# Half of the DMAs of a running logsumexp moved from SyncE's queue to ScalarE's

## The chip, the cores and the metric

The kernel runs on one core of a Trainium2 chip. A core has five engines that run their own instruction streams and meet at semaphores: TensorE (matrix multiply, into PSUM), VectorE, ScalarE (activation functions), GpSimd and SyncE, which computes nothing and here only issues DMAs. Sixteen DMA engines move data between HBM and the on-chip SBUF (128 partitions). SyncE and ScalarE can each issue DMAs through a hardware queue of their own; the issuing instruction hands the transfer over and the engine goes on, while the transfer runs. An engine executes its instructions in order: one that waits holds up all behind it.

The metric is the time of one execution on the device in microseconds. Three runs of the kernel before gave 1262.69, 1262.9 and 1263.4 us; the median is 1262.9.

## The reference

`x` has the shape (4, 4096, 4128) in float32: 4 batches, 4096 time steps, 4128 columns. The output is the running logsumexp along time, for each batch and column:

```python
out[:, 0, :] = x[:, 0, :].copy()
for t in range(1, S):
    mx = np.maximum(out[:, t - 1, :], x[:, t, :])
    out[:, t, :] = mx + np.log(np.exp(out[:, t - 1, :] - mx) + np.exp(x[:, t, :] - mx))
```

That is log(cumsum(exp(x))) along time. Input and output are 270.5 MB each, and each byte has to be moved once.

## The kernel before

**Tiles.** The work is cut into 44 steps (`steps`, lines 185 to 195), each with one tile of its own, so that "tile 21" is that of step 21. A step takes 384 consecutive time rows of one batch, all 4128 columns; 4096 = 10 x 384 + 256, so each batch has ten steps of three rows a partition (`r` = 3) and one of two (`r` = 2, first in batch 0, last in the others). Counting from 0, the two-row steps are 0, 21, 32 and 43. Partition p holds `r` consecutive time rows, a contiguous piece of HBM of 49,536 bytes (33,024 in a two-row step). One DMA loads a whole step (`Step.load`, line 127), one stores it (`Step.store`, line 130). Results are written in place: the tile `xt` is loaded, replaced by its exponentials in float16 (in half of the same bytes) and then by the logarithms in float32, and stored. Four such buffers exist (`bufs = 4`).

**Chunks.** A step is cut into four chunks of 1024 columns; the fourth has the tail of 32 columns too. For each chunk:

- `exp` (line 142, ScalarE): exponentials of all `r` rows of the chunk in one instruction.
- `head` (lines 92 and 96, TensorE): matrix products with triangular constants add up, in PSUM, the exponentials of all earlier rows of the step for row j = 0, and the carry from the step before (`pick` times `carry`).
- `stage(j)` (line 175, ScalarE): the logarithm of the PSUM sum goes to the tile as the output of row j. Then, for j + 1 < r, TensorE adds the next row's exponentials (`ident`). After the last row `keep` (lines 106 and 107, VectorE) saves the new carry. The tail's 32 columns have a logarithm of their own (line 180) behind stage 0 of the fourth chunk.

**Order.** The order is written out by hand (`tc.manual_schedule()`); the framework adds the semaphores. The main loop (line 205) goes through rounds g. Round g does stage 2 of chunk g - 2, stage 1 of chunk g - 1 and stage 0 of chunk g (three logarithms on ScalarE), then the exponential of chunk g + 2 and the head of chunk g + 1. When a step's last chunk has had its last stage, within the round and ahead of the remaining stages, the step is stored and the next load is issued (lines 210 to 214): with step s stored, the load of step s + 3. That load goes to the buffer of step s - 1, so it waits until the store of step s - 1 has landed. By then the exponentials of step s + 1 are all done but the last chunk's; ScalarE needs step s + 2 in the round after.

**Queues.** All loads and stores are issued by SyncE (`nc.sync.dma_start`) on one hardware queue, in the order store s, load s + 3, store s + 1, load s + 4. The first four loads are issued at the start. In the profile the exponentials are L142, the logarithms L175 and L180, loads L127, stores L130. Where a line of code calls TensorE through the helper `mm`, the profile has L92 (with a change of weights) or L96.

Of the kernel before, what the change touches and what calls it, by code (L numbers as in the profile page):

```python
# [49 lines left out]
def kernel(  # L50
# [11 lines left out]
    nc = tc.nc  # L62
# [49 lines left out]
    class Step:  # L112
# [7 lines left out]
            rows = t[self.b, self.row:self.row + P * self.r, :]  # L120
            return rows.rearrange("(p j) d -> p j d", j=self.r)

        def load(self):
            full = xpool.tile([P, R, D], FP32, name="xt")
            self.xt = full[:, :self.r, :]
            self.half = self.xt.bitcast(FP16)
            nc.sync.dma_start(out=self.xt, in_=self.dram(x))  # L127

        def store(self):
            nc.sync.dma_start(out=self.dram(out), in_=self.xt)  # L130

    class Chunk:
        def __init__(self, step, c):
# [51 lines left out]
    steps = []  # L185
# [10 lines left out]

    chunks = [Chunk(s, c) for s in steps for c in range(n_main)]
    ahead = bufs - 1
    for s in steps[:bufs]:
        s.load()  # L200
    stored = 0
    chunks[0].exp()
    chunks[1].exp()
    chunks[0].head()
    for g in range(len(chunks) + R - 1):
        for d in range(R - 1, -1, -1):
            if 0 <= g - d < len(chunks) and d < chunks[g - d].t.r:
                k = chunks[g - d]
                k.stage(d)
                if k.c == last and d + 1 == k.t.r:  # L210
                    k.t.store()
                    if bufs <= stored + ahead < len(steps):
                        steps[stored + ahead].load()
                    stored += 1
        if g + 2 < len(chunks):
            chunks[g + 2].exp()
        if g + 1 < len(chunks):
            chunks[g + 1].head()
# [30 lines left out]
```

## Time and profile before

| | |
|---|---|
| median of three runs | 1262.9 us |
| span of the profiled execution, first to last instruction | 1261.0 us |
| moved to and from HBM | 541 MB, 429 GB/s over the span |
| ScalarE busy | 947.0 us |
| TensorE busy | 690.7 us |
| VectorE busy | 451.4 us |
| a load of a three-row step, issue to landing (median of 40) | 42.2 us |
| a store of a three-row step, issue to landing (median of 40) | 28.1 us |
| exp of one chunk, ScalarE (mean of 176) | 2.72 us |
| log of one row of one chunk, ScalarE (mean of 512) | 1.03 us |

The profiled execution has no time of its own besides its span; the 1.9 us between the span and the median of the runs lie outside the first and last instruction, or are the difference between executions.

How to read the lines: an instruction line names its place in the program (L142), the engine, the operation and the tiles, output first. "SPq" is SyncE's queue of instructions, which here are all DMA issues. A transfer's landing is the time when the last of the 16 DMA engines reports its part done. "A <- B" in a table of waits says that A stood idle until B was done. The DMA share is the mean busy share of the 16 DMA engines.

### The profile page before, as it was taken

Reading aid. Unit: us, or ns where it says so; the run is one execution under the profiler, and the core shown is the slowest. Engines: PE = TensorE matmul, PEld = TensorE weight load, DVE = VectorE, ACT = ScalarE, POOL = GpSimd, SP = SyncE. Lnnn points to the kernel's source line nnn. Section 1 sums busy time; section 2 is a strip of 40 time slices with the busy share of each in tenths; the row PEclk is TensorE's granted clock in tenths of the full one; section 3 lists DMA queues with packets and bytes.
Section 4 is the critical chain, followed back from the end, with each engine's and each line's share of the span. In section 5 each row is a group of like instructions: output and inputs, shape, how many; then the busy total and the mean of one; then the engine's idle time right before and its main releaser. Section 6 shows DMA issues by size and latency. Waiting matters only on the chain.

```text
span 1261.0 us, 6165 instructions
## 1 busy us (share of the span) xinstructions
PE 690.7 (55%) x2268; PEld 236.3 (19%) x2268; DVE 451.4 (36%) x445; ACT 947.0 (75%) x733; POOL 2.2 (0%) x13
## 2 busy tenths in 40 slices
PE   3666545565565555555346655555534755555562
PEld 1222111121121111111112221211211211111120
DVE  2443333333333333334424333333442433333344
ACT  5997777777777777778569777777866977777784
POOL 0000000000000000000000000000000000000000
PEclk9987787877777777878778777777777778787776
DMA  9999999999999999999999999999999999999998
GB/s 411 411 443 428 432 429 437 431 431 434 437 429 431 431 439 431 434 427 434 436 431 433 434 431 438 430 434 432 435 431 433 437 430 434 433 434 431 433 420 348
DMA packets 12702, 541.46 MB, mean 429 GB/s; under 512 B 1408, under 2 KB 1408, under 8 KB 1408
## 3 DMA queue, kind: packets, MB, share of 16 engines
q1 hardware_dynamic: 12672, 541.07, 99.4%
q8 instruction: 18, 0.29, 0.1%
q14 instruction: 12, 0.10, 0.0%
HBM read 270.53 MB, written 270.53 MB: 429 GB/s over the span
## 4 chain that ended last, share of the span: by engine, by line
DMA 72%; ACT 19%; PE 5%; issue 2%; DVE 1%; SPq 0%; ACTq 0%
DMA xt<-in_x_dram 67%; ACT xt L142 10%; ACT xt L175 9%; DMA out_dram<-xt 5%; PE pt L96 3%; PE pt L92 2%; DVE carry L106 0%; DVE carry L107 0%; ACT xt L180 0%; SPq L130 0%; ACTq L244 0%; SPq L127 0%; ACTq L142 0%; PE qt L92 0%
## 5 line engine op out<-in xcount | busy, mean ns | idle before, releaser
L142 ACT ACTIVATE xt<-xt 128x3072 f16<-128x3072 f32 (+3 forms) x176 | 478.2, 2717 | 247.9 <-DMA xt<-in_x_dram 247.8
L175 ACT ACTIVATE xt<-pt 128x1024 f32<-128x1024 f32 x512 | 487.3, 1029 | 2.5 <-PE pt L96 0.7
L106 DVE CAST carry<-pt 32x1024 f16<-32x1024 f32 x176 | 216.5, 1230 | 760.9 <-ACT xt L175 760.7
L92 PE MATMUL pt<-xt,ident 128*128 128x512 f16 x176 | 76.6, 435 | 493.7 <-ACT xt L175 493.7
L96 PE MATMUL pt<-xt,ident 128*128 128x512 f16 x496 | 203.7, 477 | 35.4 <-ACT xt L175 34.7
L107 DVE TENSOR_TENSOR carry<-pt,carry 32x1024 f16<-32x1024 f32 x176 | 215.8, 1226 | 6.1
L96 PE MATMUL pt<-xt,excl 128*128 128x512 f16 x496 | 187.6, 496 | 0.0
L96 PEld LDWEIGHTS <-ident 128*128 128x128 f16 x496 | 51.0, 103 | 655.0 <-issue 641.3
L92 PE MATMUL pt<-xt,incl 128*128 128x512 f16 x176 | 92.2, 524 | 23.5 <-ACT xt L142 15.1
L92 PE MATMUL pt<-xt,excl 128*128 128x512 f16 x176 | 93.4, 531 | 0.0
L96 PE MATMUL pt<-xt,incl 128*128 128x512 f16 x176 | 92.9, 528 | 0.0
L96 PEld LDWEIGHTS <-excl 128*128 128x128 f16 x536 | 66.6, 124 | 104.1 <-issue 79.5
L92 PE MATMUL pt<-carry,pick 128*128 128x512 f16 x160 | 72.0, 450 | 0.0
L96 PE MATMUL pt<-carry,pick 128*128 128x512 f16 x160 | 68.5, 428 | 0.0
L180 ACT ACTIVATE xt<-qt 128x96 f32<-128x96 f32 (+1 forms) x44 | 10.9, 248 | 46.3 <-PE pt L96 46.3
L92 PEld LDWEIGHTS <-incl 128*128 128x128 f16 x220 | 22.6, 103 | 118.0 <-DVE carry L107 95.3
L92 PEld LDWEIGHTS <-excl 128*128 128x128 f16 x220 | 26.8, 122 | 36.8 <-issue 27.9
L96 PEld LDWEIGHTS <-incl 128*128 128x128 f16 x260 | 27.8, 115 | 10.9 <-issue 4.8
L92 PEld LDWEIGHTS <-pick 128*128 128x128 f16 x200 | 22.9, 114 | 30.4 <-issue 20.4
L96 PEld LDWEIGHTS <-pick 128*128 128x128 f16 x160 | 18.4, 115 | 28.6 <-issue 17.2
L92 PEld LDWEIGHTS <-ident 128*128 128x128 f16 x176 | 19.2, 109 | 22.7 <-issue 12.8
L106 DVE CAST carry_t<-qt 32x32 f16<-32x32 f32 x44 | 8.7, 197 | 26.0 <-ACT xt L180 25.8
(21 smaller groups left out, 56.5 us busy)
## 6 DMA issues: line engine op xcount, KB each, us to landing
xt<-in_x_dram SPq DMA_DIRECT2D x40, 6192.0 KB, 42.2
out_dram<-xt SPq DMA_DIRECT2D x40, 6192.0 KB, 28.1
xt<-in_x_dram SPq DMA_DIRECT2D x4, 4128.0 KB, 37.3
out_dram<-xt SPq DMA_DIRECT2D x4, 4128.0 KB, 29.6
```

The source lines that it names most:

```text
L92: nc.tensor.matmul(pt, lhsT=w, rhs=rhs, start=start, stop=stop, skip_group_check=True)
L96: pe.add_instruction(mybir.InstMatmult(name=nc.get_next_instruction_name(), ins=[pe.lower_ap(rhs), pe.lower_ap(w, for_matmul_weights=True) ...
L106: nc.vector.tensor_copy(cr[HI:HI + 32, :], pt[HI:HI + 32])
L107: nc.vector.tensor_tensor(out=cr[LO:LO + 32, :], in0=pt[HI:HI + 32], in1=cr[HI:HI + 32, :], op=mybir.AluOpType.subtract,)
L142: nc.scalar.activation(self.t.half[:, :, 2 * c0:2 * c0 + w], self.t.xt[:, :, c0:c0 + w], ACT.Exp,)
L175: nc.scalar.activation(t.xt[:, j, c * CH:(c + 1) * CH], pt, ACT.Ln)
L180: nc.scalar.activation(t.xt[:, :, t0:D], self.qt, ACT.Ln)
```

## The change

SyncE issues the first four loads and, while fewer than 22 steps are stored (`stored < half`), all stores and loads: stores 0 to 21 and loads 4 to 24. From store 22 on ScalarE issues, on its own hardware queue: stores 22 to 43 and loads 25 to 43. A store keeps its place in program order, behind the last stage of its step. A load issued by SyncE comes at the end of the stages of the same round; a load issued by ScalarE comes two rounds (two chunks) later, behind that round's three logarithms and ahead of its exponential. Nothing in the arithmetic is touched.

```diff
-        def load(self):
+        def load(self, queue):
             full = xpool.tile([P, R, D], FP32, name="xt")
             self.xt = full[:, :self.r, :]
             self.half = self.xt.bitcast(FP16)
-            nc.sync.dma_start(out=self.xt, in_=self.dram(x))
-
-        def store(self):
-            nc.sync.dma_start(out=self.dram(out), in_=self.xt)
+            queue.dma_start(out=self.xt, in_=self.dram(x))
+
+        def store(self, queue):
+            queue.dma_start(out=self.dram(out), in_=self.xt)
...
     ahead = bufs - 1
+    half = len(steps) // 2
+    queue = lambda: nc.sync if stored < half else nc.scalar
+    stored = 0
     for s in steps[:bufs]:
-        s.load()
-    stored = 0
+        s.load(nc.sync)
+    due = {}
...
                 if k.c == last and d + 1 == k.t.r:
-                    k.t.store()
+                    k.t.store(queue())
                     if bufs <= stored + ahead < len(steps):
-                        steps[stored + ahead].load()
+                        due[g if stored < half else g + 2] = (steps[stored + ahead], queue())
                     stored += 1
+        if g in due:
+            s, q = due.pop(g)
+            s.load(q)
         if g + 2 < len(chunks):
             chunks[g + 2].exp()
```

## The prediction

> **What bounds the kernel now.** I read the page first: busy times, the slices, the queues.
>
> ```profile
> span 1261.0 us, 6165 instructions
> ...
> PE 690.7 (55%) x2268; PEld 236.3 (19%) x2268; DVE 451.4 (36%) x445; ACT 947.0 (75%) x733; POOL 2.2 (0%) x13
> ...
> DMA  9999999999999999999999999999999999999998
> ...
> q1 hardware_dynamic: 12672, 541.07, 99.4%
> ```
>
> No compute engine is full; ScalarE, the fullest, works 75% of the span. The 16 DMA engines are at nine tenths or more in all slices but the last, and all 541 MB go through one hardware queue. Next come the waits: who stands still, and for what. The first line is ScalarE's, the other two are SyncE's queue.
>
> ```profile
> ACT xt L142 <- DMA xt<-in_x_dram: 247.8, 42, 11.8
> ```
>
> ```profile
> SPq L130 <- ACT xt L175: 1174.4, 44, 30.0
> SPq L127 <- DMA out_dram<-xt: 18.4, 5, 4.9
> ```
>
> ScalarE is late for nothing but loads: 247.8 us in 42 waits, 5.9 us a step. A load almost never waits for the store that frees its buffer (5 times, 4.9 us at most). Then SyncE's timeline around the middle, each line a start and a duration.
>
> ```profile
> 632.86 0.33 SPq L130 DMA_DIRECT2D out_dram<-xt  x1
> 638.10 0.34 SPq L127 DMA_DIRECT2D xt<-in_x_dram  x1
> 668.50 0.33 SPq L130 DMA_DIRECT2D out_dram<-xt  x1
> 668.93 0.38 SPq L127 DMA_DIRECT2D xt<-in_x_dram  x1
> ...
> 751.28 0.33 SPq L130 DMA_DIRECT2D out_dram<-xt  x1
> 751.71 0.38 SPq L127 DMA_DIRECT2D xt<-in_x_dram  x1
> 780.60 0.33 SPq L130 DMA_DIRECT2D out_dram<-xt  x1
> ```
>
> Counting from the first, the store at 632.86 is that of tile 21 (tiles count from 0), so 668.50 is tile 22, the first that ScalarE would issue, and 638.10 is the load of tile 24. In the steady stretch stores are 29.32 us apart (751.28 to 780.60): one store and one load, 14.65 us each. Forty such pairs and four pairs of two-row tiles (9.76 us a transfer, from the completion of store 42 at 1250.40 to that of store 43 at 1260.16) take 40 x 29.3 + 4 x 19.5 = 1250 us of the 1261. The data path is the bound, and issue order or issuer can only matter where the path runs dry. The end of the program shows such a place, in busy times by stretch (last columns: DMA share, GB/s).
>
> ```profile
> 1220.00:1230.00 10.00, 6.13 (x25) 2.28 (x25) 3.46 (x6) 8.18 (x8) 0.00 (x0) 0.83 0.89 386
> 1230.00:1240.00 10.00, 6.41 (x20) 2.06 (x20) 7.79 (x7) 9.60 (x9) 0.00 (x0) 0.83 0.63 269
> ```
>
> The mean DMA engine is idle 1.1 + 3.7 = 4.8 us there, because the engines have drifted apart: store 41 completes on its first engine at 1227.96 and on its last at 1235.55, and store 42 was issued at 1234.00. The last engine was never dry; it sets the end.
>
> **The change, part by part.** The profiled execution spans 1261.0 us; the runs' median is 1262.9. The sum is made on the span and 1.9 us are added.
>
> *First half.* Stores and loads 0 to 24 stay on SyncE (load 24 is still due at store 21). Loads now stand after the remaining stages of the same round in program order, but SyncE runs none of these: 0.
>
> *Steady second half, on the queue.* Take store 25 at 751.28. Ahead of it is load 27, which lands at 764.68 (from the trace's completion records, one for each of the 16 engines, as all landings here); store 25 then runs until 779.4. Load 28 is issued today at 751.71 and lies in the queue until then. After the change it comes two rounds later: after ScalarE has received load 27, run one exp and three logs (5.5 us; the rows at 677.02 to 682.52 below), and perhaps the tail's log, which waits 0.68 to 1.10 us for TensorE: 6.4 us in all. 764.7 + 6.4 = 771.1, plus 0.38 of issuing and 1.0 until the first bytes move (the first load of the program: issued at 0.80, first packet at 1.81) is 772.5. The path needs it at 779.4. Cover 6.9 us, cost 0. If that cover were gone, each microsecond would be paid on each of the 19 loads that ScalarE issues (25 to 43). The store that frees the buffer is issued a step earlier and lands 28.1 us after its issue (the median of the page's DMA part); ScalarE asks for it 49 us after that issue (store 24 at 722.04, load 28 at 771.1), so this wait holds nothing.
>
> *Steady second half, on ScalarE.* A store is the instruction behind the log that finishes its tile, ahead of two more logs. ScalarE stands from the end of that log: 0.04 us to the issue (the log's row of 1232.93 and 1.02 us, the store at 1234.00), 0.33 of issuing, some 0.06 to start again (the chain has 0.02 + 0.04 after a wait), and the 0.1 us by which neighbouring logs overlap today: 0.54 us. A load costs 0.38 or lies beside the tail log's wait. Together at most 0.9 us a step against 5.9 us of waiting for loads: 0. Behind ScalarE's issue stand the exp that feeds TensorE and the logs that VectorE and TensorE wait for; they are late by the same 0.9 us and wait the less for the next load. Bounds: 0 below, and above 22 x 2 issues at the longest of SyncE's (1.51 us, one of 44 loads), 3.0 us a step, still under 5.9.
>
> *The handover.* ScalarE's timeline there:
>
> ```profile
> 673.07 2.85 ACT L175 ACTIVATE xt<-pt 128x1024 f32<-128x1024 f32 x3
> 677.02 2.76 ACT L142 ACTIVATE xt<-xt 128x3072 f16<-128x3072 f32 x1 [1.10 <-DMA xt<-in_x_dram]
> 679.69 2.83 ACT L175 ACTIVATE xt<-pt 128x1024 f32<-128x1024 f32 x3
> 683.20 0.25 ACT L180 ACTIVATE xt<-qt 128x96 f32<-128x96 f32 x1 [0.68 <-PE pt L96]
> ```
>
> When store 22 enters the new queue (668.5 + 0.4 of issuing + 1.0 = 669.9), load 24 has 676.9 - 669.9 = 7.0 us left on its last engine, in the old queue. No row shows two hardware queues with work at once. The bounds: the old queue goes first, load 24 lands at 676.9 as today; or the new one goes first, and it lands when both are done, 676.9 + 14.65 = 691.6. The nearest rows are instruction fetches, which come by another queue: a 16 KB packet took 0.9 to 1.1 us among data packets that move 49.5 KB in 1.83 us, where its bytes alone would be 0.6. It did not wait for the queued data and it did not stop it: a share near half. With halves load 24 lands at 669.9 + 14.0 = 683.9. Then load 25 is issued 6.4 us later, and its bytes move at 683.9 + 6.4 + 1.4 = 691.7; load 24 and store 22 keep the path busy until 691.6. Cost 0.1 us; 0 at the lower bound; at the upper 691.6 + 7.8 - 691.6 = 7.8 us. Later steps get nothing back, the path being full. I take 0.4, a little above the halves, since a packet of 1.83 us more on store 22's side costs its full length.
>
> A rule bears on this. The Trainium skill's page "DMA: Bandwidth & Descriptors" (section "Queues, rings and completion order") says that each DMA engine takes turns between the queues it has work for, a packet at a time; no run here shows it for two data queues. By turns of single data packets the sum is that of the halves; if a packet is a whole transfer's share on one engine, as its 9 to 17 descriptors would allow, load 24 finishes first and the handover costs 0. The same page ("Issuing engines are not separate DMA queues") speaks against a gain: a second issuing engine saves only issue time, and SyncE's rows above show that time to be 0.4 us beside transfers of 14.65.
>
> *The end.* ScalarE has 1.34 us of waiting left before the exp at 1220.72, and that exp leads to store 42. Between the load it received at 1196.1 and that point it gains the issue of load 43 and store 41, 0.9 us: covered, 0. Store 42 itself goes out where it does now (1234.0), store 43 0.6 us later than 1244.5, but its bytes are wanted at 1250.4. If the cover failed, each microsecond would be a microsecond of the end.
>
> Sum: 1261.0 + 0.4 = 1261.4 span; with 1.9 around it **1263.3 us**, no change.
>
> **The rivals.** *The handover runs dry (slower).* Store 22 takes more than its half, ScalarE gets load 24 late, load 25 is issued late, all engines stop. It costs from a landing after 683.8 and passes 0.2% from 686.3; the bound is 1262.9 + 7.8 = 1270.7. For it: no margin at equal shares. Against: the fetch rows; and the last engine's remainder, 7.0 us, is small.
>
> *ScalarE's issues are dear (slower).* It decides in the last two tiles, where two issues have 1.34 us of cover; past 1.34 + 2.5 = 3.8 us, 1.9 each, the program ends over 0.2% later, at 2.5 each at 1262.9 + 3.7 = 1266.6. Against: 0.33 to 0.38 on SyncE, one at 1.51.
>
> *The engines drift otherwise (faster, or somewhat slower).* The last engine's lag grew from 4.7 us (load 24: 672.1 to 676.9) to 7.6 us in the second half, and the last but one stands 1.4 us ahead of it. If that lag comes from SyncE's queue and ScalarE's has none, the end comes 1.4 to 2.9 us earlier, 1260.0 to 1261.5; were all lag lost, 1255.3. If the new queue adds a lag to the same engine, 1264 to 1266. Against: instruction fetches hit the engines whatever queue the data take.
>
> *Nothing is done by it.* Both engines' transfers could go into one queue: 1262.9.
>
> **How the numbers follow.** Forecast 0.48, with its own range 1261.4 to 1265.3; dry handover 0.15; dear issue 0.08; drift 0.22 (0.11 faster by over 0.2%, 0.06 within, 0.05 slower); nothing done 0.07, all within. 0.2% is 2.5 us, about what a measurement of this kernel tells from no change. Faster 0.11, within 0.48 + 0.06 + 0.07 = 0.61, slower 0.15 + 0.08 + 0.05 = 0.28. The range 1260.0 to 1268.7 leaves out about a tenth on each side.
>
> **What would show it.** In the profile after: two hardware queues of about 270 MB; ScalarE's waits for loads shorter by about 0.9 us in each of the last 22 steps, and the DMA share at 1.00 there; load 24 landing near 684 and no slice below nine tenths around 690. A DMA share under 0.95 between 685 and 700 is the first rival; ScalarE without a wait before the last tile, and issues over 1 us, the second; another spread of store 41's completions, the third. The prediction is wrong if the second half's step is not 29.3 us.

## The result and the profile after

The changed kernel takes 1265.71 us (median of 11 runs, 1265.12 to 1266.6) against 1262.85 us before (median of 11). The ratio is 1.0024, with a 95% interval of 1.0016 to 1.0032: 2.9 us slower. That is about the 0.2% at which the prediction drew its line, and the interval reaches to both sides of it. The forecast of 1263.3 was 2.4 us low. The result lies in the whole range (1260.0 to 1268.7), on the side to which a chance of 0.28 was given, but just above the likeliest case's own range (1261.4 to 1265.3).

The profiled execution spans 1263.9 us, 2.9 more than before. Its page, in the parts that answer to those shown of before:

```profile
span 1263.9 us, 6085 instructions
...
PE 686.7 (54%) x2268; PEld 238.6 (19%) x2268; DVE 451.3 (36%) x445; ACT 951.4 (75%) x733; POOL 2.2 (0%) x13
...
GB/s 410 413 442 428 427 433 431 437 432 433 435 430 438 430 432 431 437 429 435 430 429 402 415 435 426 433 433 434 434 426 434 434 437 430 432 436 433 427 435 358
...
q1 hardware_dynamic: 6768, 289.56, 53.2%
q10 hardware_dynamic: 5904, 251.51, 46.2%
...
xt<-in_x_dram SPq DMA_DIRECT2D x23, 6192.0 KB, 42.2
out_dram<-xt SPq DMA_DIRECT2D x20, 6192.0 KB, 28.1
out_dram<-xt ACTq DMA_DIRECT2D x20, 6192.0 KB, 27.8
xt<-in_x_dram ACTq DMA_DIRECT2D x17, 6192.0 KB, 22.7
```

The change does what it says: a second hardware queue, q10, carries 251.5 MB. ScalarE's loads land 22.7 us after their issue instead of 42.2, because they are issued later, not because they run faster. Of the 40 slices of about 32 us two in the middle fall out of the row, 402 and 415 GB/s (the 22nd and 23rd, from 664 to 727 us). The kernel before has 433 and 434 there:

```profile
GB/s 411 411 443 428 432 429 437 431 431 434 437 429 431 431 439 431 434 427 434 436 431 433 434 431 438 430 434 432 435 431 433 437 430 434 433 434 431 433 420 348
```

The rest of the second half is about as fast as before. So the loss has a place: the handover.

ScalarE's timeline there, issues included (its queue, ACTq):

```profile
667.25 1.04 ACT L175 ACTIVATE xt<-pt 128x1024 f32<-128x1024 f32 x1
668.33 0.38 ACTq L130 DMA_DIRECT2D out_dram<-xt  x1
668.75 1.94 ACT L175 ACTIVATE xt<-pt 128x1024 f32<-128x1024 f32 x2 [0.45 <-PE pt L96]
670.57 2.85 ACT L142 ACTIVATE xt<-xt 128x3168 f16<-128x3168 f32 x1
673.45 2.85 ACT L175 ACTIVATE xt<-pt 128x1024 f32<-128x1024 f32 x3
682.40 2.76 ACT L142 ACTIVATE xt<-xt 128x3072 f16<-128x3072 f32 x1 [6.09 <-DMA xt<-in_x_dram]
685.07 2.83 ACT L175 ACTIVATE xt<-pt 128x1024 f32<-128x1024 f32 x3
689.00 0.25 ACT L180 ACTIVATE xt<-qt 128x96 f32<-128x96 f32 x1 [1.10 <-PE pt L96]
689.01 0.35 ACTq L127 DMA_DIRECT2D xt<-in_x_dram  x1
```

Store 22 is issued at 668.33 into the new queue while load 24 still runs in the old one. Load 24 lands at 682.3; before it was 676.9. ScalarE waits 6.09 us for it instead of 1.10, and reaches the issue of load 25, which stands behind the exp of that wait, only at 689.01. What the DMA engines do meanwhile is in the busy times by stretch (last columns: DMA share, GB/s), first of the changed kernel, then of the kernel before. The view counts a packet whole in the stretch in which it starts, so that a share of a short stretch can pass 1 and is only rough:

```profile
684.00:686.00 2.00, 0.00 (x0) 0.00 (x0) 0.00 (x0) 2.00 (x3) 0.00 (x0) 0.60 1.03 446
686.00:688.00 2.00, 0.96 (x3) 0.30 (x3) 1.86 (x2) 1.90 (x3) 0.00 (x0) 0.50 0.63 272
688.00:690.00 2.00, 2.00 (x6) 0.62 (x5) 0.99 (x3) 0.84 (x2) 0.00 (x0) 0.50 0.21 83
690.00:692.00 2.00, 1.87 (x6) 0.65 (x5) 0.00 (x0) 2.00 (x1) 0.00 (x0) 0.69 1.21 372
```

```profile
686.00:688.00 2.00, 0.02 (x1) 0.02 (x1) 0.95 (x1) 2.00 (x4) 0.00 (x0) 1.00 0.95 404
688.00:690.00 2.00, 1.68 (x5) 0.53 (x5) 1.51 (x2) 2.00 (x2) 0.00 (x0) 0.73 0.93 396
```

From 686 to 690 the shares give 2 x 0.37 + 2 x 0.79 = 2.3 us of idle time; with each packet record clipped at the bounds, the mean engine is idle 1.8 us from 686 to 692. Before, it has no idle time there, counted in the same way. The packet records give the rest: store 22 is through on the first engine at 687.0, load 25's first packets start at 690.0, and its packets then take 2.07 us on average, where a packet of this size takes 1.83 on a busy path. The first of each engine takes 2.61 and the last 2.83, the six between 1.83 to 1.96. Over eight packets that is another 1.9 us. Load 25 lands 3.5 us later than before (709.69 instead of 706.18). From there on everything is shifted: store 30 by 3.5, load 41 by 2.3, the last store by 2.95 us, and the last store ends the program.

### The profile page after: what moved, and what is told of

Read it like the earlier page. It is cut to its first block, busy times and chain, and to the rows that moved or that the text cites. A ratio compares the mean times of both kernels' runs of the same rounds, so it can differ in the third digit from the quotient of the medians.

```text
span 1263.9 us, 6085 instructions
## 1 busy us (share of the span) xinstructions
PE 686.7 (54%) x2268; PEld 238.6 (19%) x2268; DVE 451.3 (36%) x445; ACT 951.4 (75%) x733; POOL 2.2 (0%) x13
## 4 chain that ended last, share of the span: by engine, by line
DMA 70%; ACT 21%; PE 5%; issue 1%; DVE 1%; SPq 0%; ACTq 0%
DMA xt<-in_x_dram 68%; ACT xt L142 11%; ACT xt L175 9%; PE pt L96 3%; DMA out_dram<-xt 3%; PE pt L92 2%; DVE carry L106 0%; DVE carry L107 0%; ACT xt L180 0%; SPq L130 0%; ACTq L130 0%; SPq L127 0%; ACTq L127 0%; ACTq L142 0%; PE qt L92 0%
## 5 line engine op out<-in xcount | busy, mean ns | idle before, releaser
L92 PE MATMUL pt<-xt,ident 128*128 128x512 f16 x176 | 78.3, 445 | 504.1 <-ACT xt L175 504.1
L96 PE MATMUL pt<-xt,ident 128*128 128x512 f16 x496 | 205.0, 482 | 35.0 <-ACT xt L175 34.7
## 6 DMA issues: line engine op xcount, KB each, us to landing
xt<-in_x_dram SPq DMA_DIRECT2D x23, 6192.0 KB, 42.2
xt<-in_x_dram ACTq DMA_DIRECT2D x17, 6192.0 KB, 22.7
```

The lines of the kernel that those rows point to most:

```text
L92: nc.tensor.matmul(pt, lhsT=w, rhs=rhs, start=start, stop=stop, skip_group_check=True)
L96: pe.add_instruction(mybir.InstMatmult(name=nc.get_next_instruction_name(), ins=[pe.lower_ap(rhs), pe.lower_ap(w, for_matmul_weights=True) ...
```

## The experiments

Two theories were put against each other. **A, the handover runs dry:** load 24 shares the DMA engines with store 22, ScalarE gets it late, load 25 is issued late, the path is empty for a while; nothing else costs anything. **B, ScalarE's queue costs something:** its issues, or having a second queue, cost time throughout the second half or once. All edits are against the changed kernel; each was timed in runs beside the kernel before (1262.8 us in both groups).

### Load 25 without its delay

```diff
-due[g if stored < half else g + 2] = ...
+due[g if stored <= half else g + 2] = ...
```

> Only load 25, the first that ScalarE issues, goes back to the round of store 22; loads 26 to 43 stay two rounds later, all on ScalarE. Theory A, the handover runs dry (in the changed kernel load 24 lands at 682.3 instead of 676.9, load 25 is issued at 689.0 and the mean DMA engine stands idle for 2.3 us between 686 and 690): load 25 is in the queue at about 671, load 24 still lands near 682, the DMA share stays at 1.00 around 690, and the time is 1262.9 (1262.2 to 1263.9). Theory B, a cost of ScalarE's queue or of its issues that is paid in the whole second half or once for having a second queue: the time stays at 1265.7.

1262.7 us, ratio 1.0000 (0.9991 to 1.0009). Load 24 lands at 682.30, as late as in the changed kernel, but the path stays busy:

```profile
686.00:688.00 2.00, 0.97 (x3) 0.31 (x3) 1.87 (x2) 1.89 (x3) 0.00 (x0) 0.68 0.98 421
688.00:690.00 2.00, 2.00 (x6) 0.59 (x5) 0.98 (x3) 1.01 (x2) 0.00 (x0) 0.50 0.97 421
```

One load moved removes the whole loss, with all 22 stores and the 18 other loads still issued by ScalarE as in the changed kernel. Theory B falls in both forms. A late load 24 alone costs nothing either: load 25 lands at 705.98, 0.2 us earlier than before.

### ScalarE issues everything

```diff
-    half = len(steps) // 2
+    half = 0
...
-        s.load(nc.sync)
+        s.load(nc.scalar)
```

> ScalarE issues every load and store from the start, loads 4 to 43 two rounds later; SyncE issues none, so no handover. Theory A: nothing is dry, 1262.9 (1261.5 to 1264.5). Theory B with a cost for each of ScalarE's issues: twice the steps, twice the loss, about 1268.6. Theory B with a cost once for the second queue: 1262.9 too. If the drift of the DMA engines is smaller on ScalarE's queue (in the changed kernel the last engine's lag grows by 1.0 us from load 25 to load 41, in the kernel before by 2.3), up to 2 us less than before: 1261.

1262.47 us, ratio 0.9998 (0.9989 to 1.0007). One queue, now q10, and no handover:

```profile
q10 hardware_dynamic: 12672, 541.07, 99.5%
```

```profile
ACT xt L142 <- DMA xt<-in_x_dram: 214.5, 42, 11.0
```

The first line is from the page's DMA queues, the second from the waits. Twice the issues on ScalarE, no loss; the waits for loads shrink from 247.8 to 214.5 us in 42 waits, 0.8 us a step, about what ScalarE spends on issuing. The two rounds of delay are free in the steady stretch. No gain from less drift was to be had: store 41's completions still spread over 5.9 us.

### The handover in the steady stretch

```diff
-    half = len(steps) // 2
+    half = len(steps) // 2 + 4
```

> The handover is at store 26 instead of store 22, in the steady stretch. There load 28 has about 10 us left when store 26 begins, where load 24 had 7. Theory A: load 28 lands 8 to 10 us late (802 to 804), load 29 is issued 6.7 us after it and its first bytes move at 809 to 812, while the first DMA engine is through at 803.7: a gap of 5.5 to 7.8 us instead of 3.0, and a time of 1268 to 1271. Theory B: 18 steps on ScalarE instead of 22, a time of 1265.2 to 1265.7.

1271.19 us (5 runs, 1270.11 to 1271.8), ratio 1.0066 (1.0053 to 1.0079). Fewer steps on ScalarE, and nearly three times the loss: 8.4 us, just above the range expected by theory A. ScalarE's timeline, and the busy times by stretch:

```profile
805.00 2.76 ACT L142 ACTIVATE xt<-xt 128x3072 f16<-128x3072 f32 x1 [16.46 <-DMA xt<-in_x_dram]
807.66 2.83 ACT L175 ACTIVATE xt<-pt 128x1024 f32<-128x1024 f32 x3
811.60 0.25 ACT L180 ACTIVATE xt<-qt 128x96 f32<-128x96 f32 x1 [1.10 <-PE pt L96]
811.61 0.35 ACTq L127 DMA_DIRECT2D xt<-in_x_dram  x1
```

```profile
802.00:804.00 2.00, 0.00 (x0) 0.00 (x0) 0.00 (x0) 0.00 (x0) 0.00 (x0) 0.50 0.80 347
804.00:806.00 2.00, 0.00 (x0) 0.00 (x0) 0.00 (x0) 1.00 (x1) 0.00 (x0) 0.50 0.35 149
806.00:808.00 2.00, 0.00 (x0) 0.00 (x0) 0.00 (x0) 2.00 (x2) 0.00 (x0) 0.50 0.12 50
808.00:810.00 2.00, 0.36 (x1) 0.10 (x1) 1.26 (x2) 2.00 (x3) 0.00 (x0) 0.50 0.00 0
810.00:812.00 2.00, 2.00 (x6) 0.65 (x5) 1.31 (x2) 0.75 (x2) 0.00 (x0) 0.50 0.00 0
```

Load 28 had about 10 us left when store 26's packets could run and landed 11.0 us late (804.91 instead of 793.92): the store took its half and a little more. ScalarE stood 16.46 us, load 29 was issued at 811.61, and the mean engine was idle for 7.4 us from 802 to 814, with packets clipped at the bounds (2 x (0.20 + 0.65 + 0.88 + 1 + 1) = 7.5 us by the shares). The loss grows with what is left of the transfer that the waiting engine needs.

### Store 22 stays on SyncE

```diff
-                    k.t.store(queue())
+                    k.t.store(nc.sync if stored <= half else nc.scalar)
```

> Store 22 stays on SyncE's queue, behind load 24; load 25, two rounds later, is the first transfer that ScalarE issues, the rest as in the changed kernel. Theory A in the form that the sharing of the engines between load 24 and store 22 makes ScalarE late: load 24 lands at 676.9 again, load 25 is issued near 683.7, before the first engine is through at 686.8, and the time is 1262.9 (1262.2 to 1264). If the two rounds of delay alone make the path dry, or theory B holds: 1265 to 1266.

1262.74 us, ratio 1.0000 (0.9991 to 1.0009). Load 24 lands at 677.14, load 25 is issued at 683.83, two rounds later as in the changed kernel, and the path is full:

```profile
686.00:688.00 2.00, 0.19 (x1) 0.00 (x0) 0.03 (x1) 2.00 (x3) 0.00 (x0) 1.00 1.00 429
688.00:690.00 2.00, 1.09 (x3) 0.35 (x3) 1.97 (x2) 2.00 (x3) 0.00 (x0) 0.61 1.00 421
```

There is still a handover with two queues at work: now store 22 shares with load 25, and lands 5.6 us late (697.23). Nobody waits for a store, so this costs nothing. The loss needs both parts, the sharing and the delay; and the sharing must hit the transfer that is waited for.

### Loads one round later instead of two

```diff
-due[g if stored < half else g + 2] = ...
+due[g if stored < half else g + 1] = ...
```

> As the changed kernel, but ScalarE's loads come one round later instead of two, so that each stands ahead of the exp that waits for the load before it, not behind it. Theory A: load 24 still lands near 682, but load 25 is issued at about 676, whether load 24 has landed or not; the path is not dry at 686.8, and the time is 1262.9 (1262.2 to 1263.9). Theory B: 1265.7.

1262.85 us, ratio 1.0001 (0.9992 to 1.0009). Load 24 lands at 682.48, late again; load 25 had been issued before ScalarE began to wait for it, at 673.62, beside a running logarithm:

```profile
673.61 1.02 ACT L175 ACTIVATE xt<-pt 128x1024 f32<-128x1024 f32 x1
673.62 0.35 ACTq L127 DMA_DIRECT2D xt<-in_x_dram  x1
674.53 1.93 ACT L175 ACTIVATE xt<-pt 128x1024 f32<-128x1024 f32 x2
682.56 2.76 ACT L142 ACTIVATE xt<-xt 128x3072 f16<-128x3072 f32 x1 [6.09 <-DMA xt<-in_x_dram]
```

The same wait of 6.09 us as in the changed kernel, and no loss. What matters is on which side of the waiting exp the issue stands.

### The handover at store 33, for the part of an instruction fetch

The last engine of load 25 was 1.9 us behind the last but one, and an instruction fetch had held one engine from 689.8 to 691.1, when load 25 should have begun. Was part of the 2.9 us this coincidence? Store 33 offers the same handover, a tile after a two-row tile, without a fetch near.

```diff
-    half = len(steps) // 2
+    half = 3 * len(steps) // 4
```

> The handover is at store 33, one tile after a two-row tile, as at store 22. Load 35 has 5 us left when the new queue's first packets can run (issue at 981.5 and the 3.4 us that store 22 took to its first packet), load 24 had 5.1. Theory A: load 35 lands 5 us late (995.4), load 36 is issued near 1002.1, moves from 1003.1, and the mean DMA engine is idle for 2 to 3 us between 999 and 1003. At store 22 the last engine of load 25 was one that an instruction fetch held from 689.8 to 691.1; it landed 1.9 us behind the last but one. No fetch falls near 1003. If the fetch had its part in the loss: 1264.0 to 1264.9; if it had none: 1265.5 to 1266.2. Theory B, a cost per step on ScalarE, 11 instead of 22: 1264.3; it expects no idle stretch near 1000.

1265.69 us, ratio 1.0022 (1.0014 to 1.0031): a loss of the same size, with no fetch near the handover. The path is dry as expected (load 35 lands at 995.87, load 36 is issued at 1002.56, and with packets clipped at the bounds the mean engine is idle 3.0 us from 996 to 1006):

```profile
996.00:998.00 2.00, 0.00 (x0) 0.00 (x0) 0.00 (x0) 2.00 (x1) 0.00 (x0) 0.50 0.91 396
998.00:1000.00 2.00, 0.00 (x0) 0.00 (x0) 0.34 (x1) 2.00 (x3) 0.00 (x0) 0.50 0.57 248
1000.00:1002.00 2.00, 1.41 (x4) 0.35 (x3) 1.97 (x2) 1.46 (x2) 0.00 (x0) 0.50 0.29 124
```

But load 36 lands only 1.7 us late and load 37 3.0; the profiled execution (span 1264.7, the slowest of the 11) ends 3.75 us later than before. So the loss is not complete when the path is full again. Load 36 completes on all engines within 1.2 us, where the spread had been 6.1 us before; a transfer that starts on an empty path takes away the lead that 15 engines had on the last one, and a delay of any single engine then makes the transfer late. This reading agrees with the spreads but was not tested by a run of its own. The trace has one such delay: an instruction fetch from 1036.88 to 1037.83 stands, by the times of the packets around it, on the engine that lands load 37 last, 1.4 us behind the next. In the kernel before, a fetch at the same place (1035.98 to 1037.04) made nothing late: load 37 landed 14.6 us after store 34, as usual. So a loss needs no fetch at the handover, but how much of it fetches make behind a restart stays open.

At store 22 the fetch was probably not on the engine that landed load 25 last. The packet records carry no engine number, but 14 engines start load 25 between 690.00 and 690.36, one at 691.06 and one at 692.09, and the last of these lands last. Behind the other 16 KB fetches that this trace has on a busy path, the next packet starts 0.01 to 0.02 us before the fetch's recorded end, and 691.06 fits that, the fetch ending at 691.07.

### All loads on SyncE, all stores on ScalarE

```diff
-    half = len(steps) // 2
+    half = len(steps)
...
-                    k.t.store(queue())
+                    k.t.store(nc.scalar)
```

> SyncE issues all loads, ScalarE all stores, from the start; no load is put off. Two queues have work side by side all the time. Theory A, each queue gets half: in the steady stretch no loss, since the next load is always queued behind the running one; but at the end load 43 shares with store 41 and lands up to 10 us after 1220.6, the last tile is computed that much later, store 42 (13.4 us after that landing) finds the path dry, and the time is 1266 to 1273. If two queues at once cost nothing: 1262.9; if they cost bandwidth in every step, 0.5 us a step or more: over 1280.

1265.23 us in the median, but spread from 1263.87 to 1280.01 over 12 runs, three of them over 1270; ratio 1.0038 (1.0014 to 1.0061). The profiled execution:

```profile
q1 hardware_dynamic: 6336, 270.54, 49.8%
q10 hardware_dynamic: 6336, 270.54, 49.7%
...
xt<-in_x_dram SPq DMA_DIRECT2D x40, 6192.0 KB, 34.7
out_dram<-xt ACTq DMA_DIRECT2D x40, 6192.0 KB, 37.4
```

Two queues side by side all the time cost no bandwidth (433 GB/s from 300 to 600 us, as before). The chain expected at the end shows, at a third of its size. Load 43 landed 3.1 us late (1223.73), not up to 10; in the steady state, too, loads came mostly 3 to 4 us late, and it was the stores that paid (mostly 11 to 14 us late). The last tile is computed that much later, and store 42 goes out at 1236.91 instead of 1234.00, 13.2 us behind that landing:

```profile
1223.81 1.91 ACT L142 ACTIVATE xt<-xt 128x2048 f16<-128x2048 f32 x1
1236.91 0.34 ACTq L130 DMA_DIRECT2D out_dram<-xt  x1
```

Store 41 was through on its last engine at 1236.78, so store 42 found the path dry, and the program's last store lands 2.6 us later than before. The median lies just under the expected range because load 43 was less late than reckoned. Why three executions took 5 to 15 us more than the median stays open; no profile was taken of one.

## Why the prediction was right or wrong

**Right: where the loss can arise, and that it arises nowhere else.** The prediction laid out the steady second half and gave it 0: cover of 6.9 us for the delayed load, 0.9 us of ScalarE against 5.9 us of waiting. All-ScalarE measured 0 for 44 steps, and 0.8 us a step of waits gone. A store's stop on ScalarE was put at 0.54 us; in the timeline the logarithm ends at 668.29 and the next begins at 668.75, 0.46, or 0.56 with the 0.1 of lost overlap (the row names TensorE for the wait, but the issue stands between). The wait for the freed buffer held nothing, as said. The end was covered, too: 0.32 us of ScalarE's wait before the last tile were left of 1.34.

**Right in mechanism: the first rival.** "Store 22 takes more than its half, ScalarE gets load 24 late, load 25 is issued late, all engines stop." Halves were near: load 24 landed at 682.3, the sum by halves was 683.9 (store 22's first packets came at 671.8 instead of 669.9, when 5.1 us of load 24 were left instead of 7.0), and load 25 came 6.7 us after it, for 6.4 predicted. So store 22 did not even have to take more than its half.

**Wrong: the term that priced it.** The handover's step was "Cost 0.1 us", from "load 24 and store 22 keep the path busy until 691.6", and 0.4 was taken. Measured, the handover cost 3.5 us at load 25 and 2.95 at the end. The step compared load 25's first bytes with the end of the last engine. But 16 engines run their shares independently and had drifted apart by 4.9 us (store 22 completes from 686.8 to 691.6 in the kernel before): the path starts to empty at 686.8. The prediction knew the drift and used it for the end of the program alone. And it let a transfer restart from an empty path at full speed; load 25's packets took 2.07 us instead of 1.83, 1.9 us for its eight. The engine that lands load 25 last pays for both: it starts at 692.09, 1.1 us after store 22's very last packet ended (691.03), and two of its packets take 3.08 and 3.29 us. For the same reasons the threshold of that rival, a landing after 683.8 to cost anything and after 686.3 to pass 0.2%, was too late: 682.3 cost 2.9 us.

**The rule weighed there** was the Trainium skill's "DMA: Bandwidth & Descriptors", section "Queues, rings and completion order": each DMA engine takes turns between its queues. The two readings of a turn gave 0 and the halves. The runs decide for turns of single packets. When store 22's first packets start, from 671.8 on, an engine has none, one or two data packets of load 24 left, and behind them the 4-byte packet that reports its part done. Seven engines report load 24 from 674.57 to 675.55, seven from 677.70 to 679.23, two at 681.54 and 682.32: these had to let one, two or three packets of store 22 go first, 1.83 us each. The reporting packet waits for a turn of its own. On the last engine three turns are 5.5 us, and load 24 was 5.4 us late; the 11.0 us of load 28 fit six turns. The instruction fetches that the prediction read as a share near half are turns too: in the kernel before, the packet of 16 KB that runs from 687.70 to 688.66 starts as a data packet ends and ends as one starts, within 0.02 us, and so do the other fetches of that size on a busy path. The page's other sentence, that a second issuing engine saves only issue time, held: all on ScalarE, or split by direction, nothing was gained.

**The other rivals.** Dear issues: no, 0.34 to 0.38 us on ScalarE in the changed kernel, with one exception in an experiment (below). Drift otherwise: the last engine's lag at store 41 fell from 7.6 to 5.4 us, but behind a restart that had cost more than that, 3.5 us at load 25; no gain from it. (The lag at load 24 before is 4.8 us by the two times given for it, not 4.7.) Nothing done by it: no, two queues.

The likeliest case got 0.48 and the dry handover 0.15. That the result lies in the whole range is owed to the rivals that widened it, not to the step that made the forecast. With the first engine's end in place of the last's, the sum by halves would have been 691.7 - 686.8 = 4.9 us of gap on the first engine and the rival would have been the forecast.

## What to carry to other kernels

A path that is always busy has no single moment at which it needs the next transfer: reckon from the engine that is through first, not from the last completion. When transfers move to a second queue, look at what is still queued in the first: here it ran at half speed from then on, and if the issue of the next transfer stands in program order behind a wait for it, the path empties; put the issue ahead of the wait (one round earlier was enough), or let the first transfer in the new queue be one that does not compete with what is waited for. The handover cost once here, and the more the more was left in the old queue: 2.9 us for 5 us of remainder, at two places, and 8.4 us for 10 us.

## What the runs showed of the hardware that was not expected

- The first packets of store 22 in the new queue started at 671.8, 3.1 us after its issue had ended (668.33 + 0.38), on engines that were busy with the old queue's packets. On an empty path, at the start of the program, the first packet came 1.0 us after the issue began.
- With load 25 issued directly behind store 22, the issue itself held ScalarE's queue for 4.04 us, from 668.81 to 672.85, about until those first packets ran; behind it the next exp waited 2.21 us:

```profile
668.81 4.04 ACTq L127 DMA_DIRECT2D xt<-in_x_dram  x1
669.68 1.02 ACT L175 ACTIVATE xt<-pt 128x1024 f32<-128x1024 f32 x1
672.90 2.84 ACT L142 ACTIVATE xt<-xt 128x3168 f16<-128x3168 f32 x1 [2.21 <-issue]
```

  All other issues took 0.33 to 0.58 us, but for a few loads on SyncE between 0.9 and 1.5. Two issues in a row into a queue whose first transfer has not begun on busy engines can hold the issuing engine; why was not tried.
- A three-row load on an empty path took 16.5 us from first packet to the last (690.0 to 706.5 on a typical engine) instead of 14.65. Its first and its last packet are the slow ones (2.61 and 2.83 us instead of 1.83). At the start of the program before, too, the first packet of each engine is slow, 1.88 us on average where the others of that two-row load take 1.22, and so is the last of the fourth load, 2.78; why was not tried.
- In the split by direction, the waiting was not shared evenly: loads were mostly 3 to 4 us later than before, stores mostly 11 to 14, at equal bytes.
